# Asking for the late V rows as the third gather of an iteration instead of the second

## The chip, the cores and the metric

The kernel runs on one core of one Trainium2 chip. The metric is the device time of one execution in microseconds, and the time before is the median of three runs. PE is TensorE, DVE VectorE, ACT ScalarE, POOL GpSimd and SP SyncE. All gathers of table rows are issued by POOL on one software queue, which the profile calls q0; the loads of weights are issued by SP on q1.

## The reference, cut to what matters

A trunk of four layers works on 256 tokens of 1024 features. Each layer has a token mixer (HGRN2, FoX, Mamba-2 SSD, HGRN2) and then a feed-forward part of experts, each expert being one row of a table U and one row of a table V. The change is in the gathers for that part.

```
def peer_ffn(h, w_q, sub_keys, u_tab, v_tab):
    ...
        idx = jnp.take_along_axis(cand_i, pos, axis=-1)
        gates = jax.nn.softmax(top_s, axis=-1)
        u = jnp.take(u_tab, idx, axis=0)
        v = jnp.take(v_tab, idx, axis=0)
        act = jax.nn.gelu(jnp.einsum('md,mhkd->mhk', xb, u).astype(jnp.float32), approximate=False) * gates
        return jnp.einsum('mhk,mhkd->md', act.astype(xb.dtype), v)
```

For each of the 128 tokens of a block there are 8 heads with 16 experts each, so 128 U rows and 128 V rows per token, of 4 KB each. A V row whose gelu is exactly zero adds nothing.

## The kernel before

There are eight stages, one for each layer and each half of the tokens (128 tokens). A stage has 64 iterations (8 heads by 8 pairs of experts), 512 in all, numbered `i`. The 128 partitions of one gather are 64 tokens by the two experts of the pair, and `g` is 0 or 1 for the first or the second 64 tokens. In the table `uv` the U row and the V row of an expert stand side by side.

An iteration has three gathers of 128 rows:

- the **whole rows** (`fetch(i, 0)`, line 1589): U and V of group 0, 8 KB each, 1 MB together, into one of four buffers `GB`;
- the **U rows** (`fetch(i, 1)`, line 1589): U of group 1 alone, 0.5 MB, into one of three buffers;
- the **late rows** (`rest_of(i)`, line 1601): V of group 1, at most 0.5 MB, into one of three other buffers. They are asked for when the gelu of the U rows is known: `ask(i)` adds a number beyond the table to the index of each row whose gelu is zero, and the gather leaves those rows out. In the profile a gather that reads `ask` is a late one, and one that reads `ix` is of the other two kinds.

In iteration `i` DVE multiplies and sums U rows with the tokens (`dot(i, 0)`, `dot(i, 1)`, in the profile SCALAR_TENSOR_TENSOR on 128x1024), ACT takes the gelu and makes diagonal matrices `dg` and `dh` out of the gates (`scaled`, `diagonal`), and in `spread(i)` PE adds the V rows with them (`add_rows`, line 1669): first the late rows of iteration `i - 3`, with `dh`, and then the V half of the whole rows of iteration `i`, with `dg`. Each of the two is four matmul records. Behind `spread(i)` PE does a portion of the next stage's mixer (`products_`, line 259). Every engine works through its instructions in the order in which they were written.

The order of the gathers is set in `fetches(n)`, at the start of iteration `n`. It walks through the list `jobs_`, which holds for each `i` the whole rows and then the U rows. Whole rows may run up to three iterations ahead, U rows two, since that is how many buffers there are:

```
            if pairs[i][2] >= known(i) or i >= n + (NH if g else NW) and n < CLOSE - 2:
                break
            if n - 1 in asks and not g:
                rest_of(n - 1)
            fetch(i, g)
```

So iteration `n` issues the U rows of `n + 2`, the late rows of `n - 1`, and the whole rows of `n + 3`. From iteration `CLOSE - 2` (506 of 512; `CLOSE` is 508) on, the limits are lifted, and all gathers that are left are issued in a row. The last four iterations have other buffers and other gathers: 508 and 509 take whole rows for both groups, and 510 and 511 take U rows for both groups, with their V rows asked for at iteration 508 (`last_rows`, line 1610).

Each gather also waits until the one eight places before it on POOL has landed, since there are eight completion semaphores, used in turn.

Of the kernel before, what the change touches and what calls it, by code (L numbers as in the profile page):

```python
# [180 lines left out]
def trunk(ctx: ExitStack, tc: tile.TileContext, d: dict, out: bass.AP):  # L181
# [155 lines left out]
    for l in range(DEPTH):  # L337
        k = KIND[l]
        n = UNITS[UK[k]]
# [1223 lines left out]
    asks = {}  # L1563
# [17 lines left out]
    def rows(i, g):  # L1581

        if i >= CLOSE + 2:
            return at_end(4 + 2 * i - 2 * CLOSE + g)
        return HALF[NH + i % NH] if apart(i, g) else buffer(i, g)[:, D:]

    def fetch(i, g):
        s, hh, q = pairs[i]
        nc.gpsimd.indirect_dma_start(buffer(i, g), None, halved if apart(i, g) else d["uv"],  # L1589
                                     bass.IndirectOffsetOnAxis(ap=got[s, hh][0][:, g, q:q + 1], axis=0))  # L1590
# [8 lines left out]
    def rest_of(i):  # L1599

        nc.gpsimd.indirect_dma_start(rows(i, 1), None, halved, bass.IndirectOffsetOnAxis(ap=asks.pop(i), axis=0),  # L1601
                                     bounds_check=2 * DEPTH * P * P - 1, oob_is_err=False)

    def last_rows():

        ix, gs, _ = got[STAGES - 1, 7]
        vec.tensor_scalar(ix[:, :, 0:2], gs[:, :, 0, NQ - 2:], 1.0, None, op0=OP.add)
        for k in range(2):
            for g in range(2):
                nc.gpsimd.indirect_dma_start(rows(CLOSE + 2 + k, g), None, halved,  # L1610
                                             bass.IndirectOffsetOnAxis(ap=ix[:, g, k:k + 1], axis=0))

    def known(i):

        s, hh, _ = pairs[i]
        return got[s, hh][2] if (s, hh) in got else 0

    def fetches(n):

        while sent[0] < len(jobs_):  # L1620
            i, g = jobs_[sent[0]]
            if pairs[i][2] >= known(i) or i >= n + (NH if g else NW) and n < CLOSE - 2:
                break
            if n - 1 in asks and not g:
                rest_of(n - 1)
            fetch(i, g)
            sent[0] += 1
        if n - 1 in asks:
            rest_of(n - 1)
        if n == CLOSE:  # L1630
            last_rows()
# [155 lines left out]
    for s in range(STAGES):  # L1787
# [23 lines left out]
        for i in range(64 * s, 64 * s + 64):  # L1811
            now[0] = i
            new, end = i % 64 in TWICE and s > 0, i % 64 == 63 and s + 1 < STAGES
            fetches(i)
            dot(i, 0)
            scaled(i, 0)
# [52 lines left out]
```

## Time and profile before

| | |
|---|---|
| median of three runs | 3079.49 us (3078.94 to 3081.22) |
| the profiled execution | 3075.86 us |
| its span on the core | 3074.1 us |
| mean granted clock of TensorE | 0.926 |
| PE busy | 2525.9 us (82%) |
| DVE busy | 2250.9 us (73%) |
| ACT busy | 1526.2 us (50%) |
| POOL busy | 1755.1 us (57%) |
| moved by DMA | 1235.72 MB, 1039.92 MB of it by the gathers |

The span is the time from the first to the last instruction on the core; the profiled execution's own time is 1.76 us longer, and it lies 3.63 us under the median of the runs. A row of the timeline gives the start, the duration, the engine, the line, the operation, what it writes and reads, and in brackets how long the engine was idle before it and what ended that idle time. A row of the waits gives who waited for what: the sum in us, how often, and the longest wait. A row of windows gives the busy time of PE, PEld (weight loads of PE), DVE, ACT and POOL with their instructions, the granted clock, the busy share of the DMA engines and the GB/s moved.

### The profile page before, as it was taken

To read this page: it belongs to the slowest core of one execution; us is meant where nothing else is said; L and a number is where in the kernel's file an instruction comes from. 1 tells how busy PE (TensorE), PEld (TensorE's weight loads), DVE (VectorE), ACT (ScalarE), POOL (GpSimd) and SP (SyncE) were. 2 spreads that over 40 slices of the span, in tenths; PEclk is the share of its full clock that TensorE was granted. 3 is DMA by queue.
4 is the path that set the end of the run, shared out by engine and by line. 5 is a ranking of instruction groups with operands and counts; after the bars stand their busy time and mean duration, and the time that the engine had idled before them with its cause. 6 is when DMAs were issued, how large, how long until landed. Compare 5 with 4: busy or idle time off the path is not lost.

```text
span 3074.1 us, 35204 instructions
## 1 busy us (share of the span) xinstructions
PE 2525.9 (82%) x9490; PEld 1109.9 (36%) x9490; DVE 2250.9 (73%) x6666; ACT 1526.2 (50%) x4410; POOL 1755.1 (57%) x1544
## 2 busy tenths in 40 slices
PE   9989787977679877899688998889878897875565
PEld 4434343332225424344233543343323253342121
DVE  1687677767876867878687787678768767787774
ACT  2465344464444643687345685346544554444333
POOL 0366465655656665655465544556556565666675
PEclk9999888998999899999899999889989999998777
DMA  7699999999999999999999999999999999999998
GB/s 313 273 410 415 417 413 415 410 416 414 411 415 401 412 411 415 381 417 415 417 401 394 403 416 417 407 414 388 416 416 414 398 415 416 408 404 413 395 414 342
DMA packets 249460, 1235.72 MB, mean 402 GB/s; under 512 B 35985, under 2 KB 36625, under 8 KB 160560
## 3 DMA queue, kind: packets, MB, share of 16 engines
q0 software_dynamic: 221184, 1039.92, 84.0%
q1 hardware_dynamic: 28080, 193.55, 15.3%
q8 instruction: 78, 1.28, 0.2%
q14 instruction: 118, 0.97, 0.1%
HBM read 1266.23 MB, written 1.05 MB: 412 GB/s over the span
## 4 chain that ended last, share of the span: by engine, by line
DMA 43%; PE 28%; DVE 16%; ACT 3%; issue 3%; POOL 1%; POOLq 0%; DVEq 0%; ACTq 0%
DMA arena<-in_uv,ix 23%; DMA arena<-in_uv,ask 21%; PE pj L1669 12%; PE pj L259 12%; DVE arena L219 9%; PE ps L259 3%; DVE cs L219 1%; ACT L232 1%; ACT dots L232 1%; PE ps L263 1%; DVE ti L219 1%; DVE si L219 1%; DVE ts L219 1%; DVE ask L219 1%; DVE sv L219 1%
## 5 line engine op out<-in xcount | busy, mean ns | idle before, releaser
L219 DVE SCALAR_TENSOR_TENSOR arena<-arena 128x1024 f32<-128x1024 f32 (+3 forms) x1282 | 1305.5, 1046 | 449.5 <-DMA arena<-in_uv,ix 440.2
L1669 PE MATMUL pj<-arena,dh 128*64 128x512 f32 x2048 | 1122.3, 676 | 497.0 <-DMA arena<-in_uv,ask 451.2
L1589 POOL DMA_INDIRECT arena<-in_uv,ix x1024 | 1089.7, 1064 | 640.1 <-issue 160.2
L1669 PE MATMUL pj<-arena,dg 128*64 128x512 f32 x2048 | 1126.6, 678 | 31.7 <-ACT dg L232 31.5
L1601 POOL DMA_INDIRECT arena<-in_uv,ask x508 | 656.4, 1292 | 657.9 <-PE pj L1669 257.2
L232 ACT ACTIVATE dots<-dots 128x1 f32<-128x1 f32 x1024 | 204.6, 200 | 1312.2 <-DVE arena L219 1310.7
L1669 PEld LDWEIGHTS pj<-arena,dh 128*64 128x64 f32 x2048 | 260.6, 148 | 1078.7 <-issue 515.4
L259 PE MATMUL pj<-arena 128*128 128x128 f32 (+1 forms) x1752 | 509.7, 439 | 1.5 <-ACT arena L232 0.8
L232 ACT ACT_TABLE_LOAD x332 | 426.0, 1283 | 6.2 <-DVE arena L219 0.8
L259 PE MATMUL pj<-raw,arena 128*128 128x512 f32 x808 | 389.0, 616 | 3.5 <-DMA raw<-in_ssm 2.6
L259 PEld LDWEIGHTS pj<-arena 128*128 128x128 f32 x1752 | 258.1, 192 | 261.0 <-issue 240.6
L1669 PEld LDWEIGHTS pj<-arena,dg 128*64 128x64 f32 x2048 | 261.4, 149 | 165.6 <-issue 81.5
L259 PEld LDWEIGHTS pj<-raw,arena 128*128 128x128 f32 x808 | 145.2, 193 | 242.3 <-issue 221.9
L232 ACT ACTIVATE dg<-dg,dots 128x64 f32<-128x64 f32 x512 | 178.1, 348 | 16.6
L232 ACT ACTIVATE dh<-m,dots 128x64 f32<-128x64 f32 x508 | 168.9, 332 | 4.2 <-PE pj L1669 4.2
L232 ACT ACTIVATE dg<-m,gs 128x64 f32<-128x64 f32 x512 | 170.1, 332 | 0.0
L219 DVE TENSOR_SCALAR dots<-dots 128x1 f32<-128x1 f32 x508 | 76.5, 151 | 123.3 <-ACT dots L232 123.0
L232 ACT ACTIVATE dots<-dots,gs 128x1 f32<-128x1 f32 x508 | 149.5, 294 | 16.5
L259 PE MATMUL ps<-arena 128*128 128x128 f32 (+6 forms) x1120 | 145.9, 285 | 2.7 <-ACT arena L1253 1.3
L259 PEld LDWEIGHTS ps<-arena 128*128 128x128 f32 (+3 forms) x1120 | 112.7, 168 | 78.6 <-issue 40.5
L219 DVE SCALAR_TENSOR_TENSOR ask<-dots,gs 128x1 int32<-128x1 f32 x508 | 81.2, 160 | 17.5
L219 DVE MAX8 sv<-arena 128x8 f32<-128x128 f32 x256 | 61.3, 280 | 31.5 <-ACT arena L1239 17.9
(130 smaller groups left out, 1783.8 us busy)
## 6 DMA issues: line engine op xcount, KB each, us to landing
raw<-in_ssm SPq DMA_DIRECT2D x48, 1024.0 KB, 9.1
raw<-in_hg SPq DMA_DIRECT2D x35, 1024.0 KB, 9.1
arena<-in_wq SPq DMA_DIRECT2D x28, 1024.0 KB, 9.0
arena<-in_hg SPq DMA_DIRECT2D x27, 1024.0 KB, 13.5
arena<-in_uv,ix POOLq DMA_INDIRECT x1028, 12.4
raw<-in_fox SPq DMA_DIRECT2D x14, 1024.0 KB, 9.3
arena<-in_fox SPq DMA_DIRECT2D x9, 1024.0 KB, 12.9
raw<-in_wq SPq DMA_DIRECT2D x8, 1024.0 KB, 10.0
```

The source lines that it names most:

```text
L219: return getattr(nc.vector, name)(o, *a, **k)
L232: nc.scalar.activation(o, i, f, **k)
L259: nc.tensor.matmul(o, w, m, start=start, stop=stop)
L263: nc.tensor.transpose(o, i, ident)
L1589: nc.gpsimd.indirect_dma_start(buffer(i, g), None, halved if apart(i, g) else d["uv"], bass.IndirectOffsetOnAxis(ap=got[s, hh][0][:, g, q: ...
L1601: nc.gpsimd.indirect_dma_start(rows(i, 1), None, halved, bass.IndirectOffsetOnAxis(ap=asks.pop(i), axis=0), bounds_check=2 * DEPTH * P * P ...
L1669: nc.tensor.matmul(accs[s][e][g * 64:g * 64 + 64], diags[i, g], rows(i, g)[:, e * 512:(e + 1) * 512], start=False, stop=hh == 7 and q == N ...
```

## The change

The two lines that put the late rows ahead of the whole rows go away. The call behind the loop, which was there before, then issues them after all other gathers of the iteration.

```
--- before.py
+++ after.py
@@ -1621,8 +1621,6 @@
             i, g = jobs_[sent[0]]
             if pairs[i][2] >= known(i) or i >= n + (NH if g else NW) and n < CLOSE - 2:
                 break
-            if n - 1 in asks and not g:
-                rest_of(n - 1)
             fetch(i, g)
             sent[0] += 1
         if n - 1 in asks:
```

No instruction is added or removed. On POOL the steady part reads before, in the middle of the program (`ask` marks late rows, 128x2048 whole rows, 128x1024 with `ix` U rows; DMASW is the landing of the gather eight places earlier):

```order
L1589 DMA arena<-in_uv,ix 128x1024 [waits DMASW4_49,DVE_49]
L1601 DMA arena<-in_uv,ask 128x1024 [waits DMASW5_49,DVE_49,PE_49]
L1589 DMA arena<-in_uv,ix 128x2048 [waits DMASW6_49,PE_49]
L1589 DMA arena<-in_uv,ix 128x1024 [waits DMASW7_49,DVE_49]
L1601 DMA arena<-in_uv,ask 128x1024 [waits DMASW0_49,DVE_49,PE_49]
L1589 DMA arena<-in_uv,ix 128x2048 [waits DMASW1_49,PE_49]
```

and after, at the same place:

```order
L1589 DMA arena<-in_uv,ix 128x1024 [waits DMASW4_49,DVE_49]
L1589 DMA arena<-in_uv,ix 128x2048 [waits DMASW5_49,PE_49]
L1601 DMA arena<-in_uv,ask 128x1024 [waits DMASW6_49,DVE_49]
L1589 DMA arena<-in_uv,ix 128x1024 [waits DMASW7_49,DVE_49]
L1589 DMA arena<-in_uv,ix 128x2048 [waits DMASW0_49,PE_49]
L1601 DMA arena<-in_uv,ask 128x1024 [waits DMASW1_49,DVE_49]
```

The late and the whole rows have changed places. The wait for PE stands on the whole rows now, and is one for the later half of PE's step: the whole rows of `n + 3` take the buffer that the `dg` matmuls of `spread(n - 1)` read, while the late rows take one that its `dh` matmuls read.

The end of the program on POOL before, from the second gather of iteration 506 on (the first late gather is that of iteration 505):

```order
L1601 DMA arena<-in_uv,ask 128x1024 [waits DMASW3_49,DVE_49,PE_49]
L1589 DMA arena<-in_uv,ix 128x2048 [waits DMASW4_49,PE_49]
L1589 DMA arena<-in_uv,ix 128x2048 [waits DMAHW1_49,DMASW5_49,Pool_49]
L1589 DMA arena<-in_uv,ix 128x1024 [waits DMASW6_49]
L1589 DMA arena<-in_uv,ix 128x1024 [waits DMAHW4_49,DMASW7_49]
L1589 DMA arena<-in_uv,ix 128x1024 [waits DMASW0_49]
L1589 DMA arena<-in_uv,ix 128x1024 [waits DMAHW6_49,DMASW1_49]
L1601 DMA arena<-in_uv,ask 128x1024 [waits DMASW2_49,DVE_49,PE_49]
```

and after:

```order
L1589 DMA arena<-in_uv,ix 128x2048 [waits DMASW3_49,DVE_49,PE_49]
L1589 DMA arena<-in_uv,ix 128x2048 [waits DMAHW1_49,DMASW4_49,Pool_49]
L1589 DMA arena<-in_uv,ix 128x1024 [waits DMASW5_49]
L1589 DMA arena<-in_uv,ix 128x1024 [waits DMAHW4_49,DMASW6_49]
L1589 DMA arena<-in_uv,ix 128x1024 [waits DMASW7_49]
L1589 DMA arena<-in_uv,ix 128x1024 [waits DMAHW6_49,DMASW0_49]
L1601 DMA arena<-in_uv,ask 128x1024 [waits DMASW1_49,DVE_49]
L1601 DMA arena<-in_uv,ask 128x1024 [waits DMASW2_49,DVE_49,PE_49]
```

Here the late rows of iteration 505 have moved behind six gathers instead of one, because iteration 506 issues everything that is left. The other engines keep their order.

More of the change, by code (lines that the diff above doesn't have):

```diff
@@ L1623, in fetches @@
                 break
-            if n - 1 in asks and not g:
-                rest_of(n - 1)
             fetch(i, g)
```

## The prediction

> **What bounds the kernel.** I read the page's slices first, then the chain, the waits, the two gather lines and the timeline of an iteration and of the end.
>
> ```profile
> DMA  7699999999999999999999999999999999999998
> GB/s 313 273 410 415 417 413 415 410 416 414 411 415 401 412 411 415 381 417 415 417 401 394 403 416 417 407 414 388 416 416 414 398 415 416 408 404 413 395 414 342
> ...
> q0 software_dynamic: 221184, 1039.92, 84.0%
> ...
> DMA 43%; PE 28%; DVE 16%; ACT 3%; issue 3%; POOL 1%; POOLq 0%; DVEq 0%; ACTq 0%
> ...
> L1589 POOL DMA_INDIRECT arena<-in_uv,ix x1024 | 1089.7, 1064 | 640.1 <-issue 160.2
> ...
> L1601 POOL DMA_INDIRECT arena<-in_uv,ask x508 | 656.4, 1292 | 657.9 <-PE pj L1669 257.2
> ```
>
> From the third slice to the 39th the transfers run at 381 to 417 GB/s, and 417 is the best. Summed over these 37 slices of 76.85 us, the shortfall against 417 is 275 GB/s, so 275 / 417 x 76.85 = 51 us. That is all that any order of the same gathers could win between the start and the end. Bytes don't change. So the order matters only where it lets the queue run empty, and at the start and the end, where nothing else covers a wait.
>
> ```profile
> PE pj L1669 <- DMA arena<-in_uv,ask: 451.2, 224, 9.7
> DVE arena L219 <- DMA arena<-in_uv,ix: 440.2, 256, 5.4
> PEld pj L1669 <- ACT dg L232: 348.9, 192, 5.4
> POOL arena L1601 <- PE pj L1669: 257.2, 205, 5.0
> ...
> POOL arena L1601 <- DMA arena<-in_uv,ix: 153.8, 92, 4.1
> ...
> POOL arena L1589 <- PE pj L1669: 4.0, 8, 1.0
> ```
>
> PE waits for late rows in 224 of the iterations and DVE for whole or U rows in 256: both run right behind the transfers, so these waits are what a full queue looks like and not 891 us to be won. POOL in turn asks for late rows when PE has finished with their buffer (205 times) or when a gather eight places back has landed (92 times).
>
> An undisturbed iteration, near the end, without mixer work:
>
> ```profile
> 3025.57 0.61 PE L1669 MATMUL pj<-arena,dh 128*64 128x512 f32 x1 [2.82 <-DMA arena<-in_uv,ask]
> ...
> 3027.89 1.06 PE L1669 MATMUL pj<-arena,dg 128*64 128x512 f32 x1
> ...
> 3027.96 1.22 DVE L219 SCALAR_TENSOR_TENSOR arena<-arena 128x1024 f32<-128x1024 f32 x1 [1.73 <-DMA arena<-in_uv,ix]
> ...
> 3028.98 1.08 POOL L1601 DMA_INDIRECT arena<-in_uv,ask  x1 [1.15 <-PE pj L1669]
> ...
> 3029.22 1.22 DVE L219 SCALAR_TENSOR_TENSOR arena<-arena 128x1024 f32<-128x1024 f32 x1
> ...
> 3030.36 0.94 POOL L1589 DMA_INDIRECT arena<-in_uv,ix  x1 [0.30 <-issue]
> ...
> 3030.61 0.61 PE L1669 MATMUL pj<-arena,dh 128*64 128x512 f32 x1 [1.66 <-DMA arena<-in_uv,ask]
> ```
>
> The landings come in the order of use: late rows at 3025.57, whole rows 2.39 us later, U rows within 1.26 us more (DVE didn't wait for them), the next late rows 1.39 us after that. PE ends 3.4 us after its late rows, and POOL then issues the late rows and the whole rows.
>
> How full the queue is shows in the time from issue to landing, on the late line and then on the other:
>
> ```profile
> DMA to landing us min/median/max: 5.3/11.4/28.0
> ```
>
> ```profile
> DMA to landing us min/median/max: 6.4/12.4/27.4
> ```
>
> A late gather needs 1.29 us to be issued and some 1.3 us to move, so in the median 11.4 - 2.6 = 8.8 us of older work lies ahead of it, and at the very least 5.3 - 2.6 = 2.7 us. I call this the reserve.
>
> **The change, steady part.** No instruction is added. Three cases, by what PE waits for:
>
> - PE waits for late rows (224 iterations). They now land behind a whole gather, 2.4 us later, and PE's step with them. The whole rows are issued that much later, but no longer behind the late issue (0.30 + 1.29 us sooner), and their place in the stream is one late gather (1.1 to 1.4 us) nearer: 2.4 - 1.6 + 1.2 = 2.0 us less reserve. The late rows are issued 2.4 + 0.30 + 0.94 = 3.6 us later for a place 2.4 us further back: 1.2 us less.
> - PE is late for another reason (most of the other 288). Then its end doesn't move. The whole rows gain 1.6 - 1.2 = 0.4 us of reserve and the late rows 2.4 - 1.24 = 1.2 us.
> - The `dg` matmuls wait for ACT and come after the `dh` matmuls (192 waits of 348.9 / 192 = 1.8 us). Today the late rows are issued in that gap; after, they and the next U rows queue on POOL behind the whole rows, which wait for `dg`: 1.24 + 1.8 - 2.4 = 0.6 us less for the late rows, up to 1.8 us less for the U rows.
>
> The cover for all of this is the reserve of 8.8 us. If it were gone, each low point of the queue would cost up to the 2.0 us. DVE's `dot` of the U rows isn't moved: whole rows come a late gather earlier, but U rows come where they came. PE's mixer portion starts up to 2.4 us later, so DVE may wait for it before its routing work; that shifts DVE against the stream and takes from the same reserve. The low points are these:
>
> ```profile
> 1268.00:1306.00 38.00, 38.00 (x119) 14.60 (x116) 35.48 (x124) 25.52 (x74) 23.24 (x22) 1.00 0.97 354
> ...
> 1614.00:1652.00 38.00, 31.28 (x83) 10.18 (x82) 30.42 (x80) 19.72 (x61) 25.16 (x23) 1.00 0.96 371
> 1652.00:1690.00 38.00, 35.30 (x123) 15.28 (x122) 27.51 (x91) 20.12 (x54) 18.91 (x17) 1.00 1.02 418
> ...
> 2383.00:2421.00 38.00, 30.96 (x82) 9.74 (x81) 32.04 (x93) 19.72 (x57) 23.40 (x21) 0.96 0.98 379
> ```
>
> A busy share of 1.02 is a full queue; at 0.96 to 0.98 it is nearly empty, and in the first of them DVE is busy 35.48 of 38 us. Ten slices of the page lie below 410 GB/s. The cost has two ends: minus 12 us, if the second case rules at the low points and gives back half of the some 25 us that they lose, and plus 20 us, if each of the ten loses the full 2.0 us. I take +2.5 us, near the middle and a little above nothing, since the smallest reserve seen (2.7 us) is still above what the change takes (2.0).
>
> **The end.** Iteration 506 issues all that is left, and the late rows of iteration 505 go behind six gathers instead of one.
>
> ```profile
> 3033.78 1.33 POOL L1601 DMA_INDIRECT arena<-in_uv,ask  x1 [1.23 <-DMA arena<-in_uv,ix]
> ...
> 3045.39 1.23 DVE L219 SCALAR_TENSOR_TENSOR arena<-arena 128x1024 f32<-128x1024 f32 x1 [1.26 <-DMA arena<-in_uv,ix]
> ...
> 3046.76 1.09 PE L1669 MATMUL pj<-arena,dh 128*64 128x512 f32 x1 [2.48 <-DMA arena<-in_uv,ask]
> ...
> 3050.29 0.35 ACT L232 ACTIVATE dh<-m,dots 128x64 f32<-128x64 f32 x1 [2.58 <-PE pj L1669]
> ...
> 3053.53 0.64 PE L1669 MATMUL pj<-arena,dh 128*64 128x512 f32 x1 [1.29 <-ACT dh L232]
> ...
> 3054.44 1.02 PE L1669 MATMUL pj<-arena,dh 128*64 128x512 f32 x2
> ...
> 3057.99 3.65 PE L1669 MATMUL pj<-arena,dh 128*64 128x512 f32 x8 [2.53 <-DMA arena<-in_uv,ask]
> ...
> 3061.57 2.84 PE L1642 MATMUL ps<-cst 128*128 128x512 f32 x6
> ...
> 3064.34 0.64 PE L1669 MATMUL pj<-arena,dg 128*64 128x512 f32 x1
> ```
>
> At 3046.76 PE gets the late rows of 505 and does `spread(508)` and `spread(509)`, until 3054.44 + 1.02 = 3055.46. At 3057.99 it gets those of 506 and does the rest: 3.65 us, three warming matmuls, 3.65 us, the end. After the change the late rows of 505 land just ahead of those of 506, at 3057.99 - 1.37 = 3056.6 (1.37 is 3046.76 - 3045.39, one late gather). That is 9.9 us later, and work that stood in front of 3057.99 now stands behind it. `spread(508)` has eight `dh` records, 3.65 us as in the last row of that kind; ACT then has to make the diagonal of 506 and those of 509 (five instructions of 0.2 to 0.35 us, 1.5 us, of which half a us lies beside PE's last records), and `spread(509)` takes some 1.9 us (3055.46 - 3053.53). So 3056.6 + 3.65 + 1.0 + 1.9 = 3063.2 in place of 3057.99: 5.2 us. The ends are 3.9 us (no gap for ACT) and 7.3 us (the 8.7 us that the block took before, with its waits and its lower clock). I take 5.5.
>
> The Trainium skill, DMA: Bandwidth & Descriptors, Anatomy of one DMA, charges a gather some 2.0 us fixed and its bytes at 436 GB/s. By it the six gathers (4.2 MB) take 9.6 us against 9.9, and 0.3 us would come off this term, 5.2 instead of 5.5. If its fixed part were paid in the row, the iteration above would last 10.8 us where it lasts 5.0, so here the trace disagrees for a queue that is kept full; it would hold at the low points, where a late gather would then be held up by 4.4 us instead of 2.4, as in the third rival.
>
> The start moves one late gather behind one whole gather, before the queue has settled; nothing there waits for late rows of the first iterations for three iterations, and I cost it at nothing.
>
> **Sum.** 5.5 + 2.5 = 8 us. The profiled execution would go from 3075.86 to 3083.9. It lies 3.63 us below the median, so the median goes from 3079.49 to 3087.5 us. Less than 0.2% (6.2 us) can't be told from no change.
>
> **The rivals.**
>
> 1. No change that shows. The second case gives back some microseconds (0 to -5) and the end costs 3.9 to 5.5: between -1 and +6 us, 3081 to 3085. For it: the low points lie where DVE or ACT is behind and PE doesn't wait for late rows. Chance 0.30.
> 2. Faster. At the low points the whole rows, 1 MB of work, enter an almost empty queue 1.6 us sooner, since they don't queue behind the late issue. That has to give back over 5.5 + 6.2 = 11.7 us, nearly half of the 25 us lost there; then 3073 us or less. Against it: in the first window DVE is full, and no order of gathers makes it faster. Chance 0.08.
> 3. Slower by much. PE in 224 iterations and DVE behind it lag by 2.4 us, the lag doesn't shrink, and the queue runs empty more often: ten low points by 2.0 us and as many new ones, 40 us at most, some 20 in the middle: 3095 to 3120. The fixed 2.0 us that the Trainium skill charges (the section cited above) would lead here too. Chance 0.20. It decides as soon as the shortest time from issue to landing of late rows falls below 2.6 us plus what they wait.
>
> That the instructions stay in their old order is excluded by POOL's order.
>
> **Chances and range.** The forecast, +6.2 to +15 us, has 0.42. Faster 0.08, same 0.30, slower 0.42 + 0.20 = 0.62. The range is 3078 to 3108: it leaves out the better half of the second rival, some of the first, and the worst part of the third. The forecast alone reaches from 3085.5 to 3094.
>
> **What the profile after would show.** POOL waits for PE on line 1589 some 250 us in place of 4.0, and hardly on line 1601; the wait of line 1601 for a landed gather is gone. PE's wait for late rows is longer, or DVE's for whole rows shorter, and the median time to landing of whole and U rows falls from 12.4 us by 1 to 2 us. The slices from the third to the 39th read as before within 10 us of shortfall. At the end PE's eight records wait for PE's own work and not for a DMA, and the span's last part, from the last gather's issue on, is 4 to 7 us longer. Wrong I would be if the shortfall of 51 us changed by more than 12 us either way, or if the end cost under 3 us because the clock or ACT's order let `spread(508)` go sooner.

## The result, and the profile after

The changed kernel takes 3101.59 us in the median of six runs (3098.49 to 3107.43), against 3080.88 us of the kernel before in six runs, three of them those that the prediction started from: a ratio of 1.0068 (95% interval 1.0057 to 1.0078), 20.7 us slower. The forecast was 8 us. The direction and the range held; one term of the sum was too small by 10 to 12 us.

The profiled execution has a span of 3099.0 us and took 3100.75 us. These are the rows of its page that answer to those shown of before: the slices, the queue, the chain, and the two gather lines. Line 1669 of before is line 1667 wherever the two lines of the change are gone.

```profile
DMA  7699999999999999999999999999999999999998
GB/s 311 255 410 410 417 414 415 413 415 411 404 409 412 413 408 415 386 416 414 412 384 391 380 416 416 403 410 387 415 415 413 391 394 416 413 396 412 404 409 325
...
q0 software_dynamic: 221184, 1039.92, 83.8%
...
DMA 35%; PE 21%; DVE 19%; issue 9%; POOL 6%; ACT 5%; another core or an unknown queue 0%; POOLq 0%; DVEq 0%; ACTq 0%
...
L1589 POOL DMA_INDIRECT arena<-in_uv,ix x1024 | 1158.0, 1131 | 1146.7 <-PE pj L1667 645.0
...
L1601 POOL DMA_INDIRECT arena<-in_uv,ask x508 | 596.7, 1175 | 163.4 <-issue 108.5
```

The bytes are the same to the last digit. From the third to the 39th slice the shortfall against 417 GB/s is now 370 GB/s in all, 370 / 417 x 77.475 = 68.7 us, where it was 50.7: 18 us more. The chain says the same in another way: it runs over transfers for 35% of the span where it was 43%, and over issue and POOL for 15% where it was 4%. So the queue of gathers is empty more often, or for longer. What POOL waits for has turned round: line 1589 waits 645.0 us for PE, where it was 4.0.

The rows of the waits, who waited for whom:

```profile
POOL arena L1589 <- PE pj L1667: 645.0, 342, 6.0
PE pj L1667 <- DMA arena<-in_uv,ask: 470.0, 215, 10.2
...
DVE arena L219 <- DMA arena<-in_uv,ix: 332.4, 250, 6.3
PEld pj L1667 <- ACT dg L232: 162.0, 89, 9.3
...
DVE dots L219 <- ACT dots L232: 139.1, 318, 7.3
...
POOL arena L1601 <- issue: 108.5, 351, 1.0
```

PE still waits for late rows (470.0 us, was 451.2). DVE waits less for transfers (332.4, was 440.2) and more for ACT (139.1, was 123.0), and PE's weight loads wait less for ACT's diagonals (162.0, was 348.9), which fits late rows that come later: PE takes them first, and the diagonals are then ready more often.

Where is the shortfall? First two windows of the kernel before, then one of after at the same place and one at a low point that the prediction showed (PE, PEld, DVE, ACT and POOL busy, the clock, the DMA engines' busy share and GB/s). After runs some 19 us behind by then, so two windows of before are shown, which take in all that it may be compared with:

```profile
2478.00:2516.00 38.00, 38.00 (x226) 23.86 (x226) 25.66 (x73) 15.29 (x52) 24.75 (x22) 1.00 1.02 415
2498.00:2536.00 38.00, 35.68 (x162) 17.23 (x162) 29.10 (x93) 18.74 (x53) 22.11 (x21) 0.96 1.02 416
```

```profile
2498.00:2536.00 38.00, 37.56 (x221) 23.40 (x221) 23.73 (x67) 13.84 (x47) 22.67 (x21) 0.96 0.96 371
1268.00:1306.00 38.00, 38.00 (x119) 14.59 (x116) 35.39 (x119) 25.08 (x71) 24.46 (x20) 1.00 0.98 358
```

The old low point at 1268 is as it was (354 before, 358 after). At 2498 a new one came up, 371 GB/s where it was 415, in a stretch in which PE is full before and after.

Another, in the timeline of after, lies between 1691 and 1729 us, where the transfers run at 377 GB/s and PE is busy for 36 of the 38 us (before: 395 GB/s at the same times, 408 eight us earlier). The gathers of after are 7.1 us behind those of before at 1568 us of before's time, and 13.9 us at 1742. PE does `spread` at 1700.85, then 7.5 us of mixer work, then the next `spread` at 1710.07:

```profile
1702.72 3.70 PE L259 MATMUL pj<-raw,arena 128*128 128x512 f32 x8
...
1703.40 1.12 POOL L1589 DMA_INDIRECT arena<-in_uv,ix  x1 [2.74 <-PE pj L1667]
...
1704.83 1.49 POOL L1601 DMA_INDIRECT arena<-in_uv,ask  x1 [0.30 <-DVE ig L219]
...
1706.35 3.78 PE L259 MATMUL ps<-fst,arena 64*128 64x64 f32 x32
...
1706.62 0.94 POOL L1589 DMA_INDIRECT arena<-in_uv,ix  x1 [0.31 <-DVE arena L219]
...
1710.07 0.64 PE L1667 MATMUL pj<-arena,dh 128*64 128x512 f32 x1
...
1713.54 0.94 POOL L1589 DMA_INDIRECT arena<-in_uv,ix  x1 [5.98 <-PE pj L1667]
...
1714.79 1.00 POOL L1601 DMA_INDIRECT arena<-in_uv,ask  x1 [0.30 <-issue]
...
1716.09 1.29 POOL L1589 DMA_INDIRECT arena<-in_uv,ix  x1 [0.31 <-issue]
```

For 5.98 us nothing is put on the queue: POOL holds the whole rows until PE has read their buffer, and the late rows and the next U rows stand behind them. PE doesn't wait here; it works. In such a stretch the kernel lives on what is on the queue when it begins: from 1708 to 1712 us the transfers still run at 422 GB/s, in the next 4 us at 320, and from 1720 to 1724 at 248. The change makes such stretches more frequent. Between 200 and 3030 us POOL's idle times ahead of gathers add up to 1153 us before and 1159 after, nearly the same, but those over 5 us are 3 before and 16 after.

The end, first a row from the timeline of before, then the timeline of after:

```profile
3053.02 1.23 DVE L219 SCALAR_TENSOR_TENSOR arena<-arena 128x1024 f32<-128x1024 f32 x1 [0.15 <-DMA arena<-in_uv,ix]
```

```profile
3064.61 1.00 POOL L1601 DMA_INDIRECT arena<-in_uv,ask  x1 [0.30 <-issue]
...
3071.03 1.23 DVE L219 SCALAR_TENSOR_TENSOR arena<-arena 128x1024 f32<-128x1024 f32 x1
...
3076.17 1.08 PE L1667 MATMUL pj<-arena,dh 128*64 128x512 f32 x1 [10.23 <-DMA arena<-in_uv,ask]
...
3079.49 1.45 PE L1667 MATMUL pj<-arena,dh 128*64 128x512 f32 x3
...
3082.06 4.46 PE L1667 MATMUL pj<-arena,dh 128*64 128x512 f32 x10
```

The `dot` at 3071.03 is that of iteration 510, the one at 3053.02 before. From there to the end were 3074.1 - 3053.02 = 21.1 us and are now 3099.0 - 3071.03 = 28.0. Its U rows come one late gather (1.3 us) earlier in the stream than before, so the end itself costs 28.0 - 21.1 - 1.3 = 5.6 us. Counted from the issue of the last gather to the end it's the same 5.6 us (18.7 before, 24.4 after). The rest of the 20.7 us, 15, is the steady part. (The two spans are 24.9 us apart, but the profiled execution of before is a quick one, 3.63 us under its median: its second slice moved 273 GB/s, while a kernel below that has the same order there moved 256. So that slice shows nothing of the change.)

### The profile page after: what moved, and what is told of

The parts are those of the page before. It is cut to its first block, busy times and chain, and to the rows that moved or that the text cites. A ratio compares the mean times of both kernels' runs of the same rounds, so it can differ in the third digit from the quotient of the medians.

```text
span 3099.0 us, 35203 instructions
## 1 busy us (share of the span) xinstructions
PE 2496.8 (81%) x9490; PEld 1109.7 (36%) x9490; DVE 2240.5 (72%) x6666; ACT 1530.0 (49%) x4410; POOL 1763.0 (57%) x1544
## 4 chain that ended last, share of the span: by engine, by line
DMA 35%; PE 21%; DVE 19%; issue 9%; POOL 6%; ACT 5%; another core or an unknown queue 0%; POOLq 0%; DVEq 0%; ACTq 0%
DMA arena<-in_uv,ask 21%; DMA arena<-in_uv,ix 14%; DVE arena L219 11%; PE pj L1667 8%; PE pj L259 8%; POOL arena L1589 4%; PE ps L259 3%; ACT L232 2%; POOL arena L1601 2%; DVE cs L219 2%; ACT dots L232 1%; DVE si L219 1%; DVE ti L219 1%; DVE ask L219 1%; DVE gs L219 1%
## 5 line engine op out<-in xcount | busy, mean ns | idle before, releaser
L1589 POOL DMA_INDIRECT arena<-in_uv,ix x1024 | 1158.0, 1131 | 1146.7 <-PE pj L1667 645.0
L219 DVE SCALAR_TENSOR_TENSOR arena<-arena 128x1024 f32<-128x1024 f32 (+3 forms) x1282 | 1301.8, 1046 | 346.8 <-DMA arena<-in_uv,ix 332.4
L1601 POOL DMA_INDIRECT arena<-in_uv,ask x508 | 596.7, 1175 | 163.4 <-issue 108.5
L219 DVE TENSOR_SCALAR dots<-dots 128x1 f32<-128x1 f32 x508 | 77.0, 152 | 149.2 <-ACT dots L232 139.1
```

What stands on the lines that cost most here:

```text
L219: return getattr(nc.vector, name)(o, *a, **k)
```

## The experiments

Three theories were held against each other for the steady part. **A**: PE's step waits for late rows that now land behind a whole gather, so it ends later, and the whole rows, which need the buffer of that step, are issued later. **B**: the late rows and the next U rows stand on POOL behind whole rows that wait for PE. **C**: PE's mixer portions come later, and ACT and DVE, which need them, lag.

**The two parts apart.** The old order until the end and the new from iteration 506 on, and the other way round:

```
-            if n - 1 in asks and not g:
+            if n - 1 in asks and not g and n < CLOSE - 2:     # tail_only: new order at the end alone
+            if n - 1 in asks and not g and n >= CLOSE - 2:    # steady_only: new order up to the end
```

> The old order up to iteration 505, the new one only from iteration 506 on (late rows of 505 behind six gathers). All theories take the end for a matter of its own: +4 to +7 us against before (ratio 1.0013 to 1.0023), 5.5 by the prediction's working. If the end were hidden, 0; if the 20.7 us all came from the end, +20.

> The new order up to iteration 505, the old one from 506 on. If the two parts add up: 20.7 - 5.5 = +15 us against before (ratio 1.005), 12 to 18. If the parts aren't independent, anything else.

Measured beside the kernel before (3081.57 us): the end alone 3085.15 us, ratio 1.0016 (1.0008 to 1.0025), so 4.9 us; the steady part alone 3094.05 us, ratio 1.0040 (1.0027 to 1.0053), so 12.3 us (8 to 16). Here and below the microseconds are worked out from the ratio; the medians differ by up to 3 us more or less. The two parts add up to 17.2 us, within the intervals of the 20.9 that the ratio 1.0068 gives for the whole. The end's term was right. The wait has its full size in the steady part alone, here in the waits of that run:

```profile
POOL arena L1589 <- PE pj L1669: 653.7, 337, 6.1
PE pj L1669 <- DMA arena<-in_uv,ask: 469.6, 224, 8.8
```

**PE takes the whole rows first.** If A holds, the step's wait for late rows should stop mattering for the whole buffer once PE does the `dg` matmuls ahead of the `dh` ones. The same edit is made in the new and in the old order, as its control:

```
+            add_rows(*((i, g) for g in range(1 + (i >= CLOSE))))
             if LAG <= i <= CLOSE:
                 add_rows((i - LAG, 1))
-            add_rows(*((i, g) for g in range(1 + (i >= CLOSE))))
```

> The new order of gathers, and in PE's step the whole rows' V half (dg) is added before the late rows (dh), so that the whole rows' buffer no longer waits for the late rows of three iterations earlier. Theory A (the buffer of the whole rows is freed later because PE waits for late rows that land behind a whole gather, and the queue is shorter by 2 us): the main part's loss mostly goes, +5 to +10 us against before. Theory B (late rows and the next U rows stand on POOL behind whole rows that wait for PE): the late rows still wait for PE there and U rows behind them, +14 to +21. Theory C (PE's mixer portions lag behind the late rows, and DVE behind them): PE still does its mixer portion only after the late rows, +14 to +21.

> The old order of gathers with the swap inside PE's step alone. The late rows stand first on POOL and wait for the dh matmuls, which now come last, so whole rows behind them gain nothing. Theory A: 0 to +4 us against before. Theory C: 0, since PE's mixer portion starts when it did. It is the control for the swap: were it faster by itself, the gain in the run with the new order would prove nothing.

Measured: 1.0049 (1.0037 to 1.0062) in the new order, 15.1 us slower than before, and 1.0019 (1.0010 to 1.0028) in the old, 5.9 us slower. By itself the first is what B and C expected (14 to 21), and the control is dearer than A expected (0 to 4). But between the two lie 9.2 us, with some 4.7 us either way, and with the end's 4.9 taken off the steady part costs 4 us instead of 12 to 15, if the swap costs the same in both orders. POOL's wait for PE, in the new order and with the swap:

```profile
PEld pj L1667 <- DMA arena<-in_uv,ask: 374.3, 186, 9.4
...
POOL arena L1589 <- PE pj L1667: 302.4, 205, 4.3
...
PE pj L1667 <- DMA arena<-in_uv,ask: 225.9, 118, 8.5
```

Half of the 645.0 us is gone, as A has it, and so is every idle time of POOL over 5 us. C isn't touched by this edit, since the mixer portion still stands behind the late rows, for which PE and its weight loads wait as much as ever; so C would have what is left, 4 us, give or take the interval. The swap isn't free: PE's step now begins with a wait for ACT's `dg`, in the old order for 450.0 us:

```profile
PE pj L1669 <- ACT dg L232: 450.0, 259, 4.8
...
POOL arena L1601 <- PE pj L1669: 264.6, 170, 5.6
```

In the new order that wait is 226.1 us, so the swap may cost less there than the 5.9 us of its control. If it cost nothing, 10 us of the steady part would be left and not 4; the run can't tell which.

**PE takes the late rows last.** To take C away, the late rows' matmuls go behind the mixer portion in 59 of each 64 iterations, in the new order and, as its control, in the old:

```
-            if LAG <= i <= CLOSE:
+            if LAG <= i <= CLOSE and not at_close(i):
...                                                            # behind products_, at the end of iteration i
+            if at_close(i):
+                add_rows((i - LAG, 1))
```

> The new order of gathers; PE adds the late rows of i-3 at the end of iteration i, behind the mixer portion, in place of ahead of the whole rows' V half (the first three and the last two iterations of a stage as before). Neither the whole rows' buffer (theory A) nor the mixer portion (theory C) then waits for the late rows of the same iteration; on POOL late rows and U rows still stand behind whole rows (theory B). A and C together: the main part's 12 to 16 us go, what stays is the end, +3 to +8 us against before. B: +12 to +21. A alone was good for some 6 us (the swap), so if C counts for nothing, +12 to +16.

> The control: the old order of gathers with the same move inside PE's program. The late rows come ahead of the whole rows on POOL and wait for dh matmuls that come later than before, so POOL can be held: A: 0 to +8 us against before. C: -5 to 0, since the mixer portion waits for nothing that lands. If it lies above the run with the new order, the order itself is not what costs, but the place of the late rows' add.

Measured: 1.0070 (1.0058 to 1.0082) in the new order, 21.6 us, so nothing came back, against the 3 to 8 expected by A and C, and just above B's 12 to 21; and 1.0139 (1.0124 to 1.0154) in the old order, 43 us, far above anything expected. The first kernel, then the second:

```profile
POOL arena L1601 <- PE pj L1667: 374.0, 242, 6.3
...
PE pj L1667 <- DMA arena<-in_uv,ask: 244.2, 118, 11.8
...
POOL arena L1589 <- PE pj L1667: 79.0, 53, 6.1
```

```profile
POOL arena L1601 <- PE pj L1669: 627.2, 314, 7.1
```

It put new waits in the place of the old: the late buffers are now freed last, and POOL stands at the late rows; and PE still waits 244.2 us for late rows, now at the end of an iteration, with the next one behind it. So it doesn't settle C, nor speak against A. It fits B as a mechanism that has a price when the wait is long enough: with the late rows second, the whole rows queue behind 627.2 us of wait, and the move costs 43 us. With the late rows third, the whole rows are out already, and the move changes next to nothing (21.6 us where the new order alone costs 20.9); what it gives back and what its own wait costs can't be told apart.

**The late rows first.** The one place that is left for them, ahead of the U rows:

```
-            if n - 1 in asks and not g:
+            if n - 1 in asks:
                 rest_of(n - 1)
             fetch(i, g)
```

> The old PE program; late rows as the first gather of an iteration, ahead of U and whole rows: late rows land one U gather (1.3 us) sooner than before, U rows and whole rows are issued behind the late rows' wait for PE. The dose in the other direction. A and C: PE gets its late rows sooner and frees buffers sooner, but U rows are asked for 1.5 to 3 us later: -3 to +4 us against before. B (a gather that waits for PE blocks what stands behind it on POOL): U rows now stand behind late rows that wait for PE, +5 to +15.

Measured: 3090.47 us, ratio 1.0032 (1.0022 to 1.0041), 9.9 us slower. That is within B's 5 to 15 and above what A and C expected (-3 to +4). Here PE's late rows are early (237.6 us of wait where it was 451.2), but POOL waits for PE (277.2 us where it was 257.2) with all three gathers of the iteration standing there:

```profile
DVE arena L219 <- DMA arena<-in_uv,ix: 460.6, 332, 6.5
POOL arena L1601 <- PE pj L1669: 277.2, 174, 6.5
PE pj L1669 <- DMA arena<-in_uv,ask: 237.6, 124, 7.3
```

So the second place, the one of the kernel before, is the best of the three, and what stands on POOL behind a gather that waits for PE can cost time.

**Nobody waits for the late rows.** The last pair asks whether the new order costs anything when no late landing holds PE up, as B by itself would have it. PE's `dh` matmuls read the V half of the whole rows of the current iteration (of iteration 508 for the last two that are late). The late rows are gathered as ever, but their values are left out of the result:

```
-    def add_rows(*todo):
+    def add_rows(*todo, of=None):
...
-                nc.tensor.matmul(..., diags[i, g], rows(i, g)[:, e * 512:(e + 1) * 512],
+                nc.tensor.matmul(..., diags[i, g], rows(*(of or (i, g)))[:, e * 512:(e + 1) * 512],
...
-                add_rows((i - LAG, 1))
+                add_rows((i - LAG, 1), of=(i, 0))
```

> The old order, and PE's dh matmuls read the V half of the current iteration's whole rows in place of the late rows. The late rows are still gathered, byte for byte, but their values aren't used, and nobody waits for their landing. POOL then issues late rows as soon as an earlier gather has landed and the index is known, and only the whole rows stand on POOL waiting for PE. This is the base for the run beside it. All theories: within 15 us of the kernel before, rather below it (3068 to 3085 us), since PE's 224 waits for late rows go away but the stream of gathers stays the bound.

> The new order with the same replacement: late rows gathered behind the whole rows, their values not used, nobody waits for their landing. If the change costs time because PE waits for late rows that land behind a whole gather (theory A), or because PE's mixer portions and ACT and DVE behind them then lag (theory C), the difference to the old order with the same replacement is 0 to 4 us, the end included, since the late rows of iteration 505 hold nobody up either. If it costs time because late rows and the next U rows stand on POOL behind whole rows that wait for PE (theory B), +8 to +16 us remain, POOL's wait for PE on line 1589 stays near 600 us, and the slices show 10 to 20 us more shortfall than the run beside it.

Measured beside the kernel before (3081.1 us): old order 3075.42 us (3072.54 to 3077.7), new order 3077.0 (3074.37 to 3078.42), both at a ratio of 0.9985 (0.9976 to 0.9994). The medians are 1.6 us apart, and the two intervals allow about 4 (the granted clock is 0.975 and 0.969, so the pair is even in that too; the kernel before had 0.92 to 0.94). The 8 to 16 us that B asked for aren't there. The waits, in the old order and then in the new:

```profile
POOL arena L1589 <- issue: 159.7, 484, 2.7
...
POOL arena L1589 <- PE pj L1669: 84.8, 58, 2.7
```

```profile
POOL arena L1589 <- PE pj L1667: 193.8, 136, 4.7
POOL arena L1589 <- issue: 160.8, 370, 3.9
```

With the very same order of gathers on POOL, its wait for PE falls from 645.0 us to 193.8 as soon as PE doesn't wait for late rows. So the change costs what it costs because PE waits for late rows that land later: the order alone has no price that these runs can see. That the price goes by the whole rows' buffer (A) is what POOL's wait and the swap say; the pair takes A and C away together, and B too where it is a link in the same chain, late and U rows held up behind whole rows that PE frees late. The slices say the same: the shortfall from the third to the 39th is 44.6 us in the old order and 47.2 in the new. Nor was the queue fuller to begin with: the older work ahead of a gather, worked out from the completion events as further below, is 9.0, 9.2 and 10.2 us in the median in the old order of the pair (whole, late and U rows), as in the kernel before, and 9.1, 10.1 and 9.2 in the new.

The profiled executions side by side. The third column is worked out from the slices as above; the last is from the trace's completion events (one for each of the 16 DMA engines that a gather runs on): the share of gathers between 200 and 3030 us for which, when their issue ended, the middle one of the engines had less than 3 us left of the gather before.

| kernel | ratio to before | shortfall, slices 3 to 39 | under 3 us left |
|---|---|---|---|
| nobody waits, old order | 0.9985 | 44.6 us | 5.9% |
| nobody waits, new order | 0.9985 | 47.2 us | 5.5% |
| before | 1 | 50.7 us | 6.3% |
| new order at the end alone | 1.0016 | 48.9 us | 5.8% |
| old order, whole rows first on PE | 1.0019 | 55.3 us | 6.1% |
| late rows first | 1.0032 | 65.5 us | 9.6% |
| new order but for the end | 1.0040 | 63.4 us | 10.0% |
| new order, whole rows first on PE | 1.0049 | 61.2 us | 6.5% |
| after | 1.0068 | 68.7 us | 9.3% |
| new order, late rows last on PE | 1.0070 | 69.8 us | 9.9% |
| old order, late rows last on PE | 1.0139 | 94.0 us | 9.5% |

The time follows the shortfall within some 5 us; the kernels with the new end carry some 5 us on top. The trace of before has nearly all of its completion events (24566 of 24576), the others lack 11 to 15% of them, so the last column is good to a point or two there. It separates most of the kernels that lost from those that didn't, but it doesn't rank them.

## Why the prediction was right and wrong, by its own steps

**The end, +5.5 us: right.** 5.6 us from the two traces, 4.9 (2.5 to 7.7) with the end alone. As forecast, `spread(508)` and `spread(509)` went behind the wait for the late rows of 505, and the eight records that waited for a DMA before are now part of a run of ten that follows PE's own work (3082.06). The 5.2 us that came with the rule of the Trainium skill (DMA: Bandwidth & Descriptors, Anatomy of one DMA) are as near to what was measured, so no run here tells the two apart.

**The steady part, +2.5 us: the term that was mis-sized.** It measured 12.3 us alone and some 15 as the rest of the whole, inside the bounds of -12 to +20. Of its three cases the first carries the cost: without a wait for late rows there is none, as the last pair shows, and POOL's wait for PE says how: PE ends its step later, and the whole rows are asked for later. The fall of the reserve was also right. For the 224 iterations I had 2.0 us less for whole rows and 1.2 for late rows; from the completion events (the time at which the last engine ends the gather before, minus the end of the issue) the median fell from 8.9 to 6.8 us for whole rows, from 9.1 to 7.8 for late and from 10.2 to 7.8 for U rows, for which I had 1.8 at most. (The kernel with the new order at the end alone, whose trace lacks as many events as that of after, has 8.9, 9.0 and 10.0.)

What failed is the step from there to a price: "the smallest reserve seen (2.7 us) is still above what the change takes (2.0)". Two things were wrong with it. The time to landing is that of the slowest of 16 DMA engines. In the trace of before the first engine is through with a gather 5.5 us ahead of the last one in the median, so that the middle engine had 5.2 us left where I counted 8.8, and under 3 us in 6.3% of the gathers; after the change the median was nearly the same, 5.0 us, but the share was 9.3%. And the reserve is spent unevenly: there are stretches in which no gather is issued for up to 6 us (the 5.98 us above; 16 of over 5 us where there were 3), and a stretch that got by on 9 us doesn't on 7. No run tells the shares of these two apart. I priced the low points that were there; those hardly moved (354 to 358 GB/s in the first), and new ones came up, as the third rival had it. For the steady part its 20 to 40 us was too much, but its mechanism was the nearer one: what I called a lag that doesn't shrink is, as I read the waits, one that the buffers' return carries to the next iteration. The measured time lies in that rival's stretch, 3095 to 3120, which I gave 0.20, and not in the forecast's own, 3085.5 to 3094. The range held because it was wide enough to take in part of the rival.

Three figures of this working were off. Of the 37 slices 11 lie below 410 GB/s, not ten, and by the same sum they lose 38 us, not some 25, so the bounds come out at -19 and +22. And the end's lower bound, without the gap for ACT, is 4.2 us by its own terms and not 3.9. The +2.5 and the 5.5 don't depend on them.

**The second rival**, faster because whole rows enter an empty queue 1.6 us sooner, didn't show: whole rows go out later, not sooner, since their buffer is what is late. **The first**, no visible change, is what comes about once PE's wait for late rows is taken away.

**What the profile would show.** POOL's wait moved to line 1589 as forecast but is 645.0 us instead of some 250: I had only moved the old wait, and not added to it that PE's step itself ends later. Line 1601's wait for a landed gather fell from 153.8 to 8.0 us, and DVE waits less for transfers. The last part of the span, from the last gather's issue on, is 5.6 us longer, inside the 4 to 7. I had named a change of the shortfall by more than 12 us as what would prove me wrong; it is 18, so by its own test the steady part was wrong while the sum stayed in the range.

**Open.** How the 12 to 15 us are shared. The swap leaves 4 us for B and C together, with 4.7 either way, or up to 10 if the swap itself costs less in the new order; the pair with the late rows last on PE couldn't tell, and with the late rows first B has a price. A fifth buffer for whole rows would be the direct test of A; it wasn't tried.

## What to carry to other kernels

In a queue of transfers that each wait for a buffer, look for the loop: a transfer moved back makes its reader late, and whatever that reader frees last is asked for later, in every iteration that waits. Price such a change by the stretches where the issuing engine is held up longest and not by the smallest reserve that a full run shows. And a time to landing is that of the slowest DMA engine; the others have less in hand.

## What was not expected of the hardware

The 16 DMA engines drift apart on a full queue. In the trace of before, the completions of one gather are spread over 5.5 us in the median (2.5 to 9 us from the 5th to the 95th percentile), more than an undisturbed iteration of 5.0 us; in that of after, where the queue runs low more often, over 3.5 us. The trace of after lacks 14% of its events, but that isn't the reason: the kernel with the new order at the end alone lacks 15% and has 5.0 us. These numbers are worked out from the completion events, and no run was made to test what sets the spread. The Trainium skill, DMA: Bandwidth & Descriptors, Latency and other measured facts, says that engines 7 and 15 are usually slower than the others; the events here don't name the engine, so the runs neither bear that out nor speak against it.
